# Seven block products for the down-projection of a SwiGLU FFN, and accumulation into DRAM

## The chip, the cores and the metric

One core of a Trainium2 chip runs the kernel. The metric is the device time of one execution in microseconds (us), as the median of several runs. TensorE (PE) multiplies, VectorE (DVE) and ScalarE (ACT) do elementwise work, GpSimd (POOL) and SyncE (SP) mostly issue transfers; 16 DMA engines move the data.

## The reference, cut to what matters

One step of a decoder trunk: a half-step FFN, a mixer of attention and state-space heads, a second half-step FFN and a last norm, over 520 tokens (512 of a prompt, 8 of single-token sequences). Only the two FFNs are touched. All is in float32.

```python
D_MODEL = 1024; D_FF = 2816
def half_ffn(x, norm_g, w_in, w_out):
    h = rmsnorm(x, norm_g)
    gate, up = jnp.split(h @ w_in, 2, axis=-1)
    return x + FFN_RESIDUAL * ((jax.nn.silu(gate) * up) @ w_out)   # FFN_RESIDUAL = 0.5
```

## The kernel before

Activations lie transposed: x is eight tiles of 128 features x 520 tokens, and the 520 tokens are handled as two halves of 260. Each float32 operand of a matmul is cut into a high part (a cast to fp32r on ScalarE) and a low part (a subtraction on VectorE), and a product is three matmuls: high x high, high x low, low x high. `cut` does this for weights, and takes two tiles of the "q" ring; raw weights come by DMA into tiles of the "r" ring.

The hidden width of 2816 is 22 tiles of 128, taken in four parts (`PARTS`): tiles 0 to 5, 6 to 11, 12 to 17, 18 to 21. Within a part the gate and up projections of its tiles come first, then the part's down-projection, which adds 0.5 times its result to x in SBUF (line 468). The first five tiles (`SFROM`) are plain: 96 matmuls each. The others are "pairs": gate and up with two halves of the model width and two token halves are a 2 x 2 block product, done with seven block products in place of eight (`comb_pair`, `comb_last`, 84 matmuls). The seven weight combinations are made from five raw tiles: two of them get their sum by an accumulating DMA from GpSimd's queue (lines 348 and 349), two more by additions on VectorE (lines 381 and 383), and then all seven are cut (lines 354 and 355). The combinations of the activations are made once per FFN by `combos`. The PSUM banks of a pair are called x, y and z; partial sums stay in a bank, are read there by ScalarE or VectorE, and further products are added to them. Product 4 of a pair is issued inside the next pair.

The down-projection (the loop over m in `ffn_comb`) is plain: for each of eight output tiles m, two banks, one for each token half, with (tiles of the part) x 3 matmuls each. Its weights are two raw tiles, 512 and 256 columns wide, for a part of six tiles. The last part of the first FFN takes its weights from the mixer's stream (`w_take`), and the last part of the second FFN is done by `last_out`.

TensorE's instructions run in the order in which the program states them. The other engines' order is worked out by a scheduler when the program is built, with the program's order as priority; on the chip each engine's order is fixed. `stream` lists the weight units with the time each is to cover; `b_more` cuts units until 10 us of work (`AHEAD`) are cut ahead, and `b_split` has raw weights loaded two units ahead. SBUF pools: "pf" (14 q tiles and 12 r tiles), "pg" (12 more q tiles), "p2" (58 general tiles of 528 columns). x is reloaded at the end of part 0, from the input xT in the first FFN and from a DRAM tensor `spill` in the second (the mixer writes its sum there).

## Time and profile before

| | |
|---|---|
| time, median of 3 runs | 1107.76 us (1106.94 to 1111.99) |
| the profiled execution's own time | 1109.26 us |
| its span from first to last instruction | 1107.5 us |
| PE, DVE, ACT, POOL busy in the span | 1073.4, 719.4, 501.4, 264.6 us |
| mean granted TensorE clock | 0.99 of full speed |
| bytes by DMA | 204.30 MB, 184 GB/s in the mean |

The busy time of an engine is the time that at least one of its instructions covers. Instructions can overlap: a matmul's duration runs from its start to its modelled end, and the next one may have started by then. The share of the DMA engines is the mean busy share of 16 engines in a stretch. The first FFN lies at 8 to 376 us, the mixer after it, the second FFN from about 715 us to the end.

### The profile page before, as it was taken

The numbers are of one execution on the slowest core, as the hardware profiler recorded it, in microseconds if no ns is written. First come the engines' busy times: TensorE is split into PE (matmuls) and PEld (weight loads), VectorE is DVE, ScalarE is ACT, GpSimd is POOL, SyncE is SP. The second block draws the span as 40 slices with busy tenths as digits, with TensorE's granted clock in tenths as the row PEclk, the third lists the DMA queues.
The fourth block names the chain that finished last, engine by engine and source line by source line (L and its number), as shares of the span: only waits on it lengthen the run. The fifth ranks groups of instructions, "written<-read, shape, count | busy, mean of one in ns | idle before, by whom it ended". The sixth has DMA issues, their size and how long they took to land.

```text
span 1107.5 us, 23255 instructions
## 1 busy us (share of the span) xinstructions
PE 1073.4 (97%) x9079; PEld 991.7 (90%) x9079; DVE 719.4 (65%) x1499; ACT 501.4 (45%) x1077; POOL 264.6 (24%) x261
## 2 busy tenths in 40 slices
PE   8999999999999999999999998999999999999995
PEld 6999999999999988776756676999999999999995
DVE  6985477467555679363768868449855764685563
ACT  6452355256244422456622555245534543562452
POOL 0001001110105667575343321120020011101013
PEclk9999999999999999999999999999999999999997
DMA  8539358455616788688899735163484584556302
GB/s 272 136 104 255 92 144 222 107 139 170 161 47 205 269 305 298 232 281 305 292 379 406 268 131 197 47 221 99 133 226 104 131 232 98 147 176 150 109 11 78
DMA packets 93917, 204.30 MB, mean 184 GB/s; under 512 B 13384, under 2 KB 21960, under 8 KB 89712
## 3 DMA queue, kind: packets, MB, share of 16 engines
q1 hardware_dynamic: 68736, 124.19, 34.4%
q0 software_dynamic: 22336, 77.08, 24.6%
q10 hardware_dynamic: 2736, 1.56, 0.5%
q8 instruction: 71, 1.16, 0.4%
q14 instruction: 38, 0.31, 0.1%
HBM read 191.78 MB, written 11.01 MB: 183 GB/s over the span
## 4 chain that ended last, share of the span: by engine, by line
PE 86%; DVE 5%; DMA 3%; issue 2%; ACT 2%; POOL 1%; ACTq 0%; DVEq 0%; SPq 0%; POOLq 0%
PE fo L223 7%; PE fo L224 7%; PE fo L222 7%; PE cx L578 6%; PE cx L577 6%; PE cx L576 6%; PE mps L222 4%; PE mps L223 3%; PE mps L224 3%; PE gu L222 3%; PE gu L224 3%; PE gu L223 3%; PE cy L576 3%; PE cy L577 3%; PE cy L578 3%; PE sps L1060 2%
## 5 line engine op out<-in xcount | busy, mean ns | idle before, releaser
L354 ACT CAST qh<-br 128x512 fp32r<-128x512 f32 (+1 forms) x310 | 168.2, 585 | 120.0 <-PE fo L223 57.5
L355 DVE TENSOR_TENSOR ql<-br,qh 128x512 fp32r<-128x512 f32 (+1 forms) x310 | 188.8, 644 | 44.1 <-ACT qh L354 19.3
L223 PE MATMUL fo<-hidl,qh 128*128 128x260 f32 x640 | 181.3, 283 | 0.8 <-DVE hidl L613 0.8
L222 PE MATMUL fo<-hidh,qh 128*128 128x260 f32 x640 | 181.1, 283 | 0.0
L224 PE MATMUL fo<-hidh,ql 128*128 128x260 f32 x640 | 180.8, 283 | 0.0
L578 PE MATMUL cx<-ch,ql 128*128 128x260 f32 x544 | 153.8, 283 | 0.0
L577 PE MATMUL cx<-cl,qh 128*128 128x260 f32 x544 | 153.6, 282 | 0.0
L576 PE MATMUL cx<-ch,qh 128*128 128x260 f32 x544 | 153.5, 282 | 0.0
L223 PEld LDWEIGHTS fo<-hidl,qh 128*128 128x128 f32 x640 | 120.4, 188 | 1.6 <-DVE hidl L613 1.5
L222 PEld LDWEIGHTS fo<-hidh,qh 128*128 128x128 f32 x640 | 120.5, 188 | 0.0
L224 PEld LDWEIGHTS fo<-hidh,ql 128*128 128x128 f32 x640 | 120.5, 188 | 0.0
L222 PE MATMUL mps<-hh,whi 128*128 128x260 f32 x384 | 113.3, 295 | 2.3 <-DVE raw L880 2.3
L348 POOL DMA_DIRECT2D br<-in_wi x34 | 29.7, 874 | 354.7 <-DMA br<-in_wi 204.7
L223 PE MATMUL mps<-hl,whi 128*128 128x260 f32 x384 | 109.7, 286 | 0.6 <-DVE hl L233 0.6
L224 PE MATMUL mps<-hh,wlo 128*128 128x260 f32 x384 | 109.4, 285 | 0.0
L576 PEld LDWEIGHTS cx<-ch,qh 128*128 128x128 f32 x544 | 102.4, 188 | 0.0
L578 PEld LDWEIGHTS cx<-ch,ql 128*128 128x128 f32 x544 | 102.4, 188 | 0.0
L577 PEld LDWEIGHTS cx<-cl,qh 128*128 128x128 f32 x544 | 102.3, 188 | 0.0
L786 POOL DMA_INDIRECT kv<-in_kc,ix x66 | 74.0, 1122 | 59.5 <-PE cy L578 25.7
L222 PEld LDWEIGHTS mps<-hh,whi 128*128 128x128 f32 x384 | 73.3, 191 | 13.5 <-issue 10.4
L577 PE MATMUL cy<-cl,qh 128*128 128x260 f32 x272 | 77.0, 283 | 0.0
L576 PE MATMUL cy<-ch,qh 128*128 128x260 f32 x272 | 76.9, 283 | 0.0
(430 smaller groups left out, 2705.4 us busy)
## 6 DMA issues: line engine op xcount, KB each, us to landing
br<-in_wi SPq DMA_DIRECT2D x206, 256.0 KB, 3.9
br<-in_wi POOLq DMA_DIRECT2D x68, 256.0 KB, 4.7
br<-in_wo SPq DMA_DIRECT2D x56, 256.0 KB, 2.9
wraw<-in_wm SPq DMA_DIRECT2D x24, 512.0 KB, 6.3
br<-in_wo SPq DMA_DIRECT2D x48, 128.0 KB, 2.7
kv<-in_kc SPq DMA_DIRECT2D x22, 256.0 KB, 4.6
spill<-xr SPq DMA_DIRECT2D x16, 260.0 KB, 3.3
xr<-spill SPq DMA_DIRECT2D x16, 260.0 KB, 5.5
```

Of the source, the lines that this page charges most:

```text
L222: mm(out, lhsT=hi[:, ks], rhs=xh[:, cs], start=start, stop=False)
L223: mm(out, lhsT=hi[:, ks], rhs=xl[:, cs], start=False, stop=False)
L224: mm(out, lhsT=lo[:, ks], rhs=xh[:, cs], start=False, stop=stop)
L348: nc.gpsimd.dma_start(s1, u[:, h[1]], accum_op=ALU.add)
L354: self.nc.scalar.copy(hi[:, :n], raw[:, :n])
L355: self.nc.vector.tensor_sub(lo[:, :n], raw[:, :n], hi[:, :n])
L576: mm(out, lhsT=hi[:, ks], rhs=xh, start=start and i == 0, stop=False, skip_group_check=True)
L577: mm(out, lhsT=hi[:, ks], rhs=xl, start=False, stop=False, skip_group_check=True)
L578: mm(out, lhsT=lo[:, ks], rhs=xh, start=False, stop=i == 3, skip_group_check=True)
L786: nc.gpsimd.indirect_dma_start(out=pages[j], out_offset=None, in_=a["kc"], in_offset=bass.IndirectOffsetOnAxis(ap=self.ix[:, 4 * n + j:4 * ...
L1060: nc.tensor.matmul(self.sbank[32 * hp:32 * hp + 32, cs], lhsT=self.qz[:, c0:c0 + 32], rhs=rhs(hp), start=(n % 16 == 0), stop=(n % 16 == 15 ...
```

## The change

The down-projection of the first three parts (`COMB`) is done with seven block products too. Two output tiles m and m + 1, two halves of the part's hidden tiles (three and three) and two token halves are the 2 x 2 blocks. The weights are combined and cut as for the gate/up pairs, 384 columns wide. The hidden tiles are combined in twos by the new `hidden` (the plain first five as well), so that `gate_up2` now returns the uncut product; the rows of `w_ffn_out` are reordered to suit (`hidden_order`). The results no longer go to x in SBUF: they are scaled by 0.5 or -0.5 into tiles of a new pool "px" and added to `spill` in DRAM by accumulating DMAs from GpSimd's queue. In the first FFN xT is copied to `spill` first. x is reloaded from `spill` only in the last part. The down-projection of a part now follows the first gate/up pair of the next part. In the gate/up pairs product 4 of the pair before moves from behind product 6 to behind product 5. The rings shrink: pf 14 to 11 q tiles and 12 to 10 r tiles, pg 12 to 9; px (4) and py (2) are new.

```diff
+COMB = (0, 1, 2)
...
+def hidden_order():
+    o = []
+    for part, (lo, hi) in enumerate(PARTS):
+        o += [j for i in range(2) for j in range(lo + i, hi, 2)] if part in COMB else range(lo, hi)
+    return o
...
+        def down(part):
+            lo, hi = PARTS[part]
+            n = 128 * (hi - lo)
+            w = [wo[m][:, lo * 128:hi * 128] for m in range(8)]
+            if part in COMB:
+                return [("pair", w[m], w[m + 1], n // 2, 1.26 * (hi - lo)) for m in range(0, 8, 2)]
+            return [("dn", w[m], n, 0.72 * (hi - lo)) for m in range(8)]
...
+                if j == lo and part - 1 in COMB:
+                    u += down(part - 1)
...
-        return (self.p0 if first else self.pf).tile([128, 512], F32, name=name, tag="r", bufs=4 if first else 12)
+        return (self.p0 if first else self.pf).tile([128, 512], F32, name=name, tag="r", bufs=4 if first else 10)
...
+                if j == 4:
+                    for _ in range(2):
+                        self.hidden(raw.pop(0), hid)
...
                     if after is not None:
+                        for k in range(8):
+                            nc.sync.dma_start(self.spill[k], self.a["xT"][k])
                         self.setup_cache()
...
+                    if j == lo and todo is not None:
+                        self.down_comb(hx, prev, hid)
+                        hx, todo, prev = [], None, None
...
+                if last:
+                    self.reload(self.spill)
...
+    def down_comb(self, hx, tail, hid):
+        nc = self.nc
+        a, b = slice(0, HF), slice(HF, T)
+        stt = nc.vector.scalar_tensor_tensor
+        for m in range(0, 8, 2):
+            w = self.b_take()
+            x, y, z = (self.bank1(n)[:, :HF] for n in ("dx", "dy", "dz"))
+            x0, x1 = (self.px.tile([128, 528], F32, name=f"xs{m + i}", tag="x") for i in range(2))
+            pu = self.t2("pu")
+            self.product(x, w, 1, True, hx)
+            nc.scalar.copy(z, x)
+            self.product(y, w, 5, True, hx)
+            nc.scalar.activation(pu[:, a], y, AF.Copy, scale=-0.5)
+            if m == 0:
+                self.comb_last(tail, hid)
+            self.product(x, w, 6, False, hx)
+            nc.scalar.activation(pu[:, b], x, AF.Copy, scale=0.5)
+            self.product(z, w, 2, False, hx)
+            nc.scalar.activation(x0[:, a], z, AF.Copy, scale=0.5)
+            self.product(x, w, 7, False, hx)
+            stt(x1[:, b], x, -0.5, pu[:, a], ALU.mult, ALU.add)
+            self.product(y, w, 3, False, hx)
+            stt(x0[:, b], y, 0.5, pu[:, b], ALU.mult, ALU.add)
+            nc.gpsimd.dma_start(self.spill[m], x0[:, :T], accum_op=ALU.add)
+            self.product(x, w, 4, False, hx)
+            nc.scalar.activation(x1[:, a], x, AF.Copy, scale=-0.5)
+            nc.gpsimd.dma_start(self.spill[m + 1], x1[:, :T], accum_op=ALU.add)
+            self.b_more()
...
+    def rings(self):
+        self.enter("pf", 11)
+        self.enter("px", 4)
+        self.enter("pg", 9, "right")
+        self.enter("py", 2, "right")
...
+        if prev is not None:
+            self.comb_last(prev, hid)
+        self.product(z, w, 2, False, self.cx)
+        nc.scalar.activation(c[:, a], z, AF.Silu)
+        self.product(x, w, 6, False, self.cx)
+        nc.scalar.copy(pu[:, b], x)
+        self.product(y, w, 3, False, self.cx)
...
+    def hidden(self, c, hx):
+        nc = self.nc
+        a, b = slice(0, HF), slice(HF, T)
+        if not hx or len(hx[-1]) > 1:
+            hx.append({0: c})
+            return
+        x0, x1 = hx.pop()[0], c
+        p1 = self.t2("p1", F32R)
+        nc.scalar.copy(p1[:, a], x0[:, a])
+        nc.vector.tensor_sub(p1[:, b], x0[:, a], p1[:, a])
+        s, t = self.t2("hs"), self.t2("ht")
+        nc.vector.tensor_sub(s[:, a], x0[:, a], x0[:, b])
+        nc.vector.tensor_sub(s[:, b], x1[:, b], x0[:, b])
+        nc.vector.scalar_tensor_tensor(t[:, a], s[:, b], -1.0, x0[:, a], ALU.mult, ALU.subtract)
+        nc.vector.scalar_tensor_tensor(t[:, b], t[:, a], -1.0, x1[:, a], ALU.mult, ALU.subtract)
+        q = self.two(s, x1, t)
+        cut = lambda i, z: [v[:, z] for v in q[i]]
+        hx.append({1: [p1[:, a], p1[:, b]], 5: cut(0, a), 7: cut(0, b), 2: cut(1, a), 3: cut(1, b), 6: cut(2, a), 4: cut(2, b)})
```

## Rows read from the trace of the kernel before

**Rows 1.** The page's busy times (us, share of the span, instructions), and the granted TensorE clock in 40 slices.

```profile
PE 1073.4 (97%) x9079; PEld 991.7 (90%) x9079; DVE 719.4 (65%) x1499; ACT 501.4 (45%) x1077; POOL 264.6 (24%) x261
...
PEclk9999999999999999999999999999999999999997
```

**Rows 2.** What TensorE waited for, longest first in total: line waited at, releaser, us in total, times, longest.

```profile
PE attps L1035 <- ACT pT L1023: 3.1, 2, 2.4
...
PE fo L223 <- DVE hidl L613: 1.2, 3, 0.5
```

**Rows 3.** Groups of instructions by line: a third of the down-projection's matmuls and its weight loads (busy us, mean ns), and one window of 30 us with counts.

```profile
L222 PE MATMUL fo<-hidh,qh 128*128 128x260 f32 x640 | 181.1, 283 | 0.0
...
L222 PEld LDWEIGHTS fo<-hidh,qh 128*128 128x128 f32 x640 | 120.5, 188 | 0.0
...
300.00:330.00 30.00, 30.00 (x252) 30.00 (x251) 16.79 (x33) 12.02 (x26) 1.73 (x2) 1.00 0.22 54
```

The columns of a window are: its us, busy us and count of PE, PEld, DVE, ACT and POOL, the granted clock, the DMA share and GB/s.

**Rows 4.** TensorE and then ScalarE in order of time inside one gate/up pair: start us, duration us, operation.

```profile
253.48 0.28 PE L578 MATMUL cx<-ch,ql 128*128 128x260 f32 x1
...
255.05 0.37 PE L576 MATMUL cz<-ch,qh 128*128 128x260 f32 x1
255.26 0.28 PE L577 MATMUL cz<-cl,qh 128*128 128x260 f32 x1
...
257.92 0.28 PE L578 MATMUL cx<-ch,ql 128*128 128x260 f32 x1
...
253.57 1.14 ACT L354 CAST qh<-br 128x512 fp32r<-128x512 f32 x2
254.62 0.37 ACT L587 COPY cz<-cx 128x260 f32<-128x260 f32 x1
...
258.24 0.38 ACT L593 COPY pu<-cx 128x260 f32<-128x260 f32 x1 [1.06 <-PE cx L578]
```

**Rows 5.** Groups by line with shapes kept apart, of VectorE and ScalarE (busy us, mean ns), and VectorE in order of time through one gate/up pair.

```profile
L355 DVE TENSOR_TENSOR ql<-br,qh 128x512 fp32r<-128x512 f32 x262 | 171.9, 686 | 39.9 <-ACT qh L354 18.2 <-issue 9.3 <-PE fo L224 6.7
L613 DVE TENSOR_TENSOR hidl<-cg,hidh 128x520 fp32r<-128x520 f32 x34 | 23.8, 699 | 17.1 <-ACT hidh L612 17.0
L355 DVE TENSOR_TENSOR ql<-br,qh 128x256 fp32r<-128x256 f32 x48 | 20.0, 418 | 4.2 <-PE cx L577 2.7 <-ACT qh L354 1.1 <-issue 0.3
...
L354 ACT CAST qh<-br 128x512 fp32r<-128x512 f32 x262 | 153.0, 619 | 96.9 <-PE fo L223 49.1 <-issue 18.8 <-DMA br<-in_wi 16.3
L354 ACT CAST qh<-br 128x256 fp32r<-128x256 f32 x48 | 19.5, 405 | 23.1 <-PE fo L223 8.3 <-DMA br<-in_wi 7.5 <-issue 5.8
...
249.48 0.43 DVE L609 SCALAR_TENSOR_TENSOR cg<-cx,cg 128x260 f32<-128x260 f32 x1 [1.79 <-PE cx L578]
250.60 0.70 DVE L613 TENSOR_TENSOR hidl<-cg,hidh 128x520 fp32r<-128x520 f32 x1 [0.69 <-ACT hidh L612]
...
254.76 3.09 DVE L355 TENSOR_TENSOR ql<-br,qh 128x512 fp32r<-128x512 f32 x5
259.67 0.43 DVE L609 SCALAR_TENSOR_TENSOR cg<-cx,cg 128x260 f32<-128x260 f32 x1 [1.82 <-PE cx L578]
```

**Rows 6.** The start of the first FFN: two windows (columns as in rows 3), and one line of VectorE in order of time, the first sum of tile pair 6.

```profile
30.00:60.00 30.00, 30.00 (x249) 29.91 (x248) 30.00 (x62) 15.71 (x29) 1.95 (x2) 1.00 0.41 110
60.00:90.00 30.00, 30.00 (x252) 30.00 (x252) 23.08 (x48) 15.64 (x35) 0.00 (x0) 1.00 0.56 183
...
97.28 0.69 DVE L381 TENSOR_TENSOR s<-br,br 128x512 f32<-128x512 f32 x1 [6.62 <-DMA br<-in_wi]
```

**Rows 7.** Windows (columns as in rows 3). In the first two only one accumulating transfer of 256 KB ran, in the third three plain ones of 256 KB, in the fourth loads of 256 and 128 KB in turn; the fifth is a long stretch of the first FFN; in the last one many transfers were queued.

```profile
303.00:308.00 5.00, 5.00 (x44) 5.00 (x43) 2.11 (x4) 0.62 (x1) 0.35 (x1) 1.00 0.35 54
315.00:319.00 4.00, 4.00 (x35) 4.00 (x35) 3.54 (x8) 3.50 (x8) 0.00 (x0) 1.00 0.39 68
310.00:315.00 5.00, 5.00 (x44) 5.00 (x43) 1.50 (x3) 2.62 (x7) 0.86 (x1) 1.00 0.49 161
263.00:270.00 7.00, 7.00 (x59) 6.94 (x59) 7.00 (x16) 6.84 (x18) 0.00 (x0) 1.00 0.65 182
120.00:240.00 120.00, 119.51 (x995) 119.27 (x994) 73.58 (x141) 57.28 (x123) 12.97 (x15) 1.00 0.57 147
580.00:606.00 26.00, 24.33 (x207) 16.86 (x209) 22.39 (x52) 7.23 (x20) 7.86 (x8) 1.00 1.02 421
```

**Rows 8.** GpSimd's accumulations (duration ns: least, median, most); DMA issues with the median us from issue to landing; and SP's queue in order of time: two writes to `spill`, and the end of the first FFN's weight loads up to the mixer's first.

```profile
L348 POOL DMA_DIRECT2D br<-in_wi x34: 856/865/1045, 34.7 to 1021.5; - x34
...
br<-in_wi POOLq DMA_DIRECT2D x68, 256.0 KB, 4.7
...
spill<-xr SPq DMA_DIRECT2D x16, 260.0 KB, 3.3
xr<-spill SPq DMA_DIRECT2D x16, 260.0 KB, 5.5
...
309.87 1.28 SPq L347 DMA_DIRECT2D br<-in_wi  x3
337.50 1.29 SPq L165 DMA_DIRECT2D wraw<-in_wo  x3
...
353.71 0.34 SPq L1440 DMA_DIRECT2D spill<-xr  x1
...
356.58 0.33 SPq L1440 DMA_DIRECT2D spill<-xr  x1
```

More of the change, by code (lines that the diff above doesn't have):

```diff
@@ L296, in stream @@
         u = []
-        for lo, hi in PARTS:
+        def down(part):
[5 more added lines that the diff above has]
+            return [("dn", w[m], n, 0.72 * (hi - lo)) for m in range(8)]
+        for part, (lo, hi) in enumerate(PARTS):
             for j in range(lo, hi):
@@ L301, in stream @@
                 else:
-                    u.append(("pair", wi[2 * j], wi[2 * j + 1], 10.1))
-            if s == "1" and hi == PARTS[-1][1]:
-                break
-            u += [("dn", wo[m][:, lo * 128:hi * 128], (hi - lo) * 128, 0.72 * (hi - lo)) for m in range(8)]
+                    u.append(("pair", wi[2 * j], wi[2 * j + 1], 512, 10.1))
+                if j == lo and part - 1 in COMB:
+                    u += down(part - 1)
+            if part not in COMB and not (s == "1" and hi == PARTS[-1][1]):
+                u += down(part)
         self.bu = u
@@ L419, in ffn_comb @@
                         self.leave("p0")
-                        self.enter("pg", 12, "right")
+                        self.enter("pg", 9, "right")
+                        self.enter("py", 2, "right")
                     self.b_more()
@@ L430, in ffn_comb @@
                         r = self.rsq_half2(norm, held)
-                        hid.append(self.gate_up2(*held, r))
+                        raw.append(self.gate_up2(*held, r))
                         held = None
@@ L437, in ffn_comb @@
                 else:
-                    hid.append(self.gate_up2(*pair, r if j < SRAW else None))
+                    raw.append(self.gate_up2(*pair, r if j < SRAW else None))
                 if j == SRAW - 1:
@@ L442, in ffn_comb @@
                     if after is not None:
+                        for k in range(8):
+                            nc.sync.dma_start(self.spill[k], self.a["xT"][k])
                         self.setup_cache()
-            prev = None
+            prev, hx, todo = None, [], None
             for part, (lo, hi) in enumerate(PARTS):
+                last = part == len(PARTS) - 1
+                comb = part in COMB
+                if part:
+                    hid = []
                 for j in range(max(lo, SFROM), hi):
-                    prev = self.comb_pair(j, prev, hid)
-                last = part == len(PARTS) - 1
-                if part == 0:
-                    self.reload(source)
+                    prev = self.comb_pair(j, prev, hx if prev and j == lo else hid, comb)
+                    if part == 0:
+                        for c in raw:
+                            self.hidden(c, hid)
+                    if j == lo and todo is not None:
+                        self.down_comb(hx, prev, hid)
+                        hx, todo, prev = [], None, None
+                if comb:
+                    hx, todo = hid, part
+                    continue
                 tail, prev = prev, None
+                if last:
+                    self.reload(self.spill)
                 if last and after is None:
@@ L486, in to_mixer @@
             self.w_split()
+    def rings(self):
+        self.enter("pf", 11)
+        self.enter("px", 4)
+        self.enter("pg", 9, "right")
+        self.enter("py", 2, "right")
     def enter(self, name, bufs, side="left"):
@@ L548, in combos @@
             c = self.cx[i]
-            c[1] = [t[:, a] for t in self.h[i]]
+            p1 = self.t2("p1", F32R)
+            for z, t in zip((a, b), self.h[i]):
+                nc.scalar.copy(p1[:, z], t[:, a])
+            c[1] = p1[:, a], p1[:, b]
             c[2], c[3] = ([t[:, z] for t in self.h[i + 4]] for z in (a, b))
@@ L567, in combos, with product @@
         halves(self.two(*tt), 6, 4)
-    def product(self, out, w, p, start):
+    def product(self, out, w, p, start, blocks):
         mm = self.nc.tensor.matmul
         hi, lo = w[p]
-        for i in range(4):
-            xh, xl = self.cx[i][p]
+        last = len(blocks) - 1
+        for i, block in enumerate(blocks):
+            xh, xl = block[p]
             ks = slice(128 * i, 128 * i + 128)
@@ L577, in product, with comb_pair @@
             mm(out, lhsT=hi[:, ks], rhs=xl, start=False, stop=False, skip_group_check=True)
-            mm(out, lhsT=lo[:, ks], rhs=xh, start=False, stop=i == 3, skip_group_check=True)
-    def comb_pair(self, j, prev, hid):
+            mm(out, lhsT=lo[:, ks], rhs=xh, start=False, stop=i == last, skip_group_check=True)
+    def comb_pair(self, j, prev, hid, comb):
         nc = self.nc
@@ L1533, in run @@
             self.spill = self.pd.tile([8, 128, T], F32, name="spill")
-            self.enter("pf", 14)
-            self.enter("pg", 12, "right")
+            self.rings()
             self.w_start()
@@ L1595, in run @@
             self.leave("pw")
-            self.enter("pf", 14)
+            self.enter("pf", 11)
+            self.enter("px", 4)
             self.b_limit = len(self.bu)
```

86 lines of the change are left out of this document (40 added, 46 removed).

## The prediction, made before the result was known

> **What bounds the kernel now.** I read the busy shares first, then what TensorE waited for, then how closely its matmuls follow each other, and last the engines and DMA that feed it. TensorE is busy for 97% of the span at full clock, VectorE for 65%, ScalarE for 45% [rows 1]. TensorE's waits are a few microseconds in all, and the only one at a down-projection is 1.2 us in three pieces [rows 2]. So in both FFNs TensorE sets the time, and a matmul less is time won as long as its inputs keep up. What one is worth has to be read with care: a matmul of 260 columns lasts 283 ns, but 252 of them start in 30 us, one each 0.12 us [rows 3]. They overlap, so the price is 0.12 us.
>
> The Trainium skill says that summed matmul time is a poor measure because matmuls are pipelined, and that summed weight-load time is a good one (Perfetto Trace Analysis, section Identifying the Most-Contended Engine). The trace agrees with the first half; by the second the removed matmuls would be worth 216 x 0.188 = 40.6 us, but the loads overlap too (252 loads of 188 ns would need 47 us of those 30), so the sum below doesn't use it.
>
> **The change: matmuls removed.** Down-projection of one part before: 8 tiles m x 2 token halves x 6 hidden tiles x 3 = 288. After: 4 pairs of m x 7 products x 3 blocks x 3 = 252. 36 less, in three parts of two FFNs: 216 x 0.12 = 25.9 us, all on TensorE's path. A pair of output tiles then takes 63 x 0.12 = 7.6 us in place of 8.6.
>
> **Hand-offs in PSUM.** The plain form evacuates two banks that nothing needs again soon. A new pair uses three banks over and over: product 6 may not enter bank x before the copy of x to z is done, product 7 not before pu is read from x, product 4 not before x1 is read from x. Each time one product of 9 matmuls, 1.08 us, lies between. The nearest rows are those of the gate/up pairs, with 12 matmuls (1.44 us) between: bank x is complete at 253.76, ScalarE is in two casts and starts the copy only at 254.62 (0.86 us late), and the first matmul into z is held by 0.09 us (0.21 to the next start, not 0.12); where ScalarE is idle it starts 0.04 us after the last matmul (257.92 + 0.28 to 258.24) [rows 4]. With 0.36 us less cover, the same lateness would cost 0.09 + 0.36 = 0.45 us, and a prompt start nothing. There are 24 x 3 = 72 such places: 0 to 32 us. I take 5, near the prompt end, since lateness up to 0.41 us is covered and a cast of 384 columns that is already running leaves at most 0.51 us to wait, on average half. The gate/up order also changes: comb_last now stands between product 5 and product 2, which wins up to 34 x 0.09 = 3 us at z, and one product instead of two covers product 7's wait; ScalarE starts that copy at once in the row, so nothing is lost. I take 1 us won.
>
> **VectorE and ScalarE.** A cut of 512 columns is 0.69 us on VectorE and 0.62 on ScalarE, of 256 columns 0.42 and 0.41; so 384 columns cost about 0.55 and 0.51 [rows 5]. A new weight pair has 7 cuts and two adds, and two evacuations on VectorE: 7 x 0.55 + 2 x 0.55 + 2 x 0.43 = 5.8 us; on ScalarE, with copies of 0.37 [rows 4], 7 x 0.51 + 5 x 0.37 = 5.4; both below 7.6. For the hidden tiles, each two of them now need five VectorE steps of 260 columns and three of 520, 5 x 0.43 + 3 x 0.70 = 4.3 us, against 2 x 0.70 before. By pitch (five cuts in a row take 3.09 us, so successive ones start some 0.08 us sooner than the duration says) that is about 1.2 us more for each gate/up pair; VectorE stood idle for 1.8 + 0.7 = 2.5 us of each 10.2 us pair [rows 5]. About 1.3 us stay, so VectorE rises to some 87% there and the q ring, cut from 26 to 20 tiles (14 per unit), still lets cuts run most of a unit ahead. No steady loss; if the cover goes, each microsecond over costs 30 pairs x 1 us.
>
> **The start of each FFN.** VectorE is full there (30.00 of 30 us) and then 23 of 30 [rows 6]. Tile pair 6 is now multiplied right after pair 5, at about 81 us instead of after eight down tiles, while in the trace its sums wait for data until 97.28 [rows 6]. Its loads move ahead of the down weights, into a stretch where DMA has room, and its 5.6 us of VectorE work take the place of down cuts done there now. 0 to 2 us for each FFN; I take 1 in all.
>
> **DMA.** An accumulating transfer of 256 KB alone takes 0.35 x 5 = 1.75 and 0.39 x 4 = 1.56 us of all 16 engines, three plain ones 0.49 x 5 = 2.45, so 1.65 and 0.82 us each [rows 7]. Alternating 256 and 128 KB loads take 4.55 us for 1.27 MB, 1.4 us per 384 KB; 192 KB then costs about 0.7. A gate/up pair costs 5 x 0.82 + 2 x 1.65 = 7.4 us of DMA. Check on before: a part is 6 x 7.4 + 8 x 1.4 = 55.6 us of DMA in 6 x 10.2 + 8 x 4.3 = 95.6 us, 0.58; the windows say 0.57 [rows 7]. A new weight pair costs 5 x 0.7 + 2 x 1.3 = 6.1, and its two accumulations into x in DRAM, for which the trace has no row, at least 2 x 0.82 (plain) and I take 2 x 1.65 (the accumulation into SBUF also reads a sum and writes it); twice that is the other bound. So 9.4 us (7.7 to 12.7) for 7.6 us of TensorE: DMA falls behind inside a down stretch. Over a part it is 6 x 7.4 + 4 x 9.4 = 82 us in 6 x 10.1 + 4 x 7.6 = 91, 0.90. In the 30 us of a stretch the loads that must arrive (half of pair 2, pair 3, the next gate/up pair and half of another, 20 us) and seven accumulations (11.6 us) make 32 us; the raw ring of 10 tiles, two units, gives some 4 us of lead. I take 0.5 us lost per stretch, 3 us in all; 0 if all is covered.
>
> **Queues.** GpSimd issues the accumulations at 0.87 us each, four per new pair, 3.5 of 7.6 us [rows 8]. Weight accumulations stand behind output accumulations there; an output one waits for evacuations and lands some 4.7 us after issue, the four x buffers of two pairs give 15 us. Output accumulations to one m are a part apart; those to different m needn't wait for each other: writes to the same DRAM tensor start 2.87 us apart though one lands in 3.3 [rows 8]. Eight copies of xT to DRAM on SP's queue (FFN1) fall where DMA share is 0.41. The reload of x moves to the end: eight transfers of 0.82 us, first landing 5.5 us after issue, on an SP queue that is empty from 311 to 337 us [rows 8]; 0 to 6 us, I take 0.
>
> **Sum.** -25.9 + 5 - 1 + 1 + 3 = -17.9 us. The profiled execution is 1109.26 us (span 1107.5), 1.5 above the median of 1107.76; 1109.3 - 17.9 = 1091.4, so 1090 us as a median.
>
> **Rivals.** (1) The hand-offs are late as at 253.76 in nearly all places: 72 x 0.45 = 32 us at most, 26 us at 0.36; the gain is gone, about 1108 us. For it: one such place is in the rows, and the casts stand ahead in ScalarE's order. Against: casts are shorter and half the evacuations in the rows start at once. (2) DMA becomes the bound in the down stretches: 9.4 us or, at the dearer accumulation, 12.7 per pair instead of 7.6, over 24 pairs 43 to 122 us lost, 6 x 4 us of it covered: 1090 - 3 + 19 to 98, 1106 to 1185; taking 10.7 (accumulation at 2.3 us), 24 x 3.1 - 24 = 50 lost, 1137 us. It turns the gain into a loss from 25.9 / 24 = 1.1 us lost per pair. For it: the share stands at 1.02 over 26 us where many transfers are queued and doesn't go beyond [rows 7], and accumulations move half as fast as loads. Against: the part as a whole asks for only 0.90. (3) The output accumulations are made to wait for each other's landing: 2 x 4.7 + 2 x 0.87 = 11.1 us per pair in GpSimd's queue, 24 x 3.5 = 84 us lost, 1174; [rows 8] speak against it.
>
> The Trainium skill has a rule that speaks for rival 2: DMAs from all queues run on the same 16 engines and interleave, so GpSimd's queue gives no bandwidth of its own (DMA: Bandwidth & Descriptors, section Issuing engines are not separate DMA queues). The trace agrees, with the share that stops near 1.0 in [rows 7] whichever queues are busy.
>
> **How the numbers follow.** My forecast, 1082 to 1101 us: 0.66. Rival 1, within half a percent: 0.15. Rival 2: 0.13, of which 0.01 still faster and 0.02 within. Rival 3: 0.03. Other losses over 0.5%: 0.03. About 0.5% is what a measurement here can tell from no change: faster is below 1102, slower above 1113. Faster 0.67, same 0.17, slower 0.16. The range reaches from 1081 (every cost at its low end: 1108 - 26 - 3 would be 1079, which takes all of them at once) to 1120, into rival 2; about 0.05 is left out below and 0.12 above.
>
> **What the profile after would show.** 216 fewer matmuls, down pairs 7.6 us apart; first matmuls of products 6, 7 and 4 without long pauses (rival 1: 0.3 us and more before them, behind casts on ScalarE); DMA share about 0.9 over parts 2 and 3, with TensorE unbroken (rival 2: share 1.0 in down stretches, VectorE's sums or ScalarE's casts waiting for loads, TensorE behind them); GpSimd not waiting from one output accumulation to the next (rival 3). The prediction is wrong if TensorE has more than 20 us of new pauses, or if pitch 0.12 us doesn't hold for products of 9.

## The result and the profile after

The changed kernel takes 1118.44 us (median of 5 runs, 1113.40 to 1119.80) against 1107.76 us: ratio 1.0085, 95% interval 1.0063 to 1.0107. It is slower by 0.85%, where 1.6% faster was forecast. A second measurement of it gave 1119.11 us (ratio 1.0096, 1.0081 to 1.0111). The profiled execution took 1118.44 us, its span is 1116.7 us against 1107.5.

The busy times of the page, to be held against [rows 1]: the 216 matmuls are gone, VectorE and ScalarE have more to do, and none is near its full span except TensorE.

```profile
PE 1060.8 (95%) x8863; PEld 971.9 (87%) x8863; DVE 807.5 (72%) x1679; ACT 597.2 (53%) x1321; POOL 348.5 (31%) x357
```

What TensorE waited for (line, releaser, us in total, times, longest; a releaser is the instruction or transfer that ended the wait). In [rows 2] the down-projection had 1.2 us in three pieces. Now its wait is the largest of all, and it is for one instruction: the evacuation of line 533, which must read bank x before product 4 may be added there.

```profile
PE dx L647 <- DVE xs L533: 20.0, 11, 5.0
PE stp L1345 <- DVE xdd L1342: 3.5, 2, 1.9
```

**Where the time went.** I cut the trace at the first matmul of each stretch and call "lost" what a stretch takes beyond its count of matmuls x 0.1197 us (an unbroken gate/up stretch of the second FFN has 492 in 58.88 us). From first to last matmul the two FFNs together took 739.6 us before and 745.2 after, the mixer between them 358.1 and 362.5; the rest is 0.8 us less. The first FFN takes 9.9 us longer than before, the second 4.3 us less. 25.9 us of matmuls went away, the six down stretches lose 30.7 us where the old ones lost 1.9, and the rest of the FFNs loses 2.7 more (1.4 of it at the first output tile of the first FFN's last part). In the down stretches the pause before product 4 makes up 22.7 us, nearly all of it in the third and fourth pair of each four. The first matmuls of products 6, 2 and 7 start 1.3 us late in all. The second matmuls of products 6, 7 and 4 start 0.06 to 0.11 us late in 60 of 72 places, 5.5 us in all, and at the full granted clock but for one, as here at a product 7 (start, duration; 0.19 us from the first to the second, then 0.12):

```profile
96.24 0.36 PE L647 MATMUL dx<-ch,qh 128*128 128x260 f32 x1
96.43 0.28 PE L648 MATMUL dx<-cl,qh 128*128 128x260 f32 x1
96.55 0.28 PE L649 MATMUL dx<-ch,ql 128*128 128x260 f32 x1
```

So the hand-offs of the banks (waits until another engine has read what further matmuls are to be added to) cost 6.8 us, and 5 to 7 us in most of the other kernels below, whatever their rings and transfers. Most of the remaining 1.2 us (0.9) are slower matmuls behind a pause, as in these rows (start, duration, idle before):

```profile
324.08 0.56 PE L647 MATMUL dx<-ch,qh 128*128 128x260 f32 x1 [5.03 <-DVE xs L533]
324.43 0.42 PE L648 MATMUL dx<-cl,qh 128*128 128x260 f32 x1
324.65 0.42 PE L649 MATMUL dx<-ch,ql 128*128 128x260 f32 x1
...
327.47 0.34 PE L647 MATMUL cx<-p,qh 128*128 128x260 f32 x1
327.64 0.28 PE L648 MATMUL cx<-p,qh 128*128 128x260 f32 x1
```

After 5.03 us of idleness matmuls start 0.22 us apart, not 0.12, up to 327.47. The granted clock is 0.50 from 324.20 to 327.40, the lower of the two clock levels (1.2 of 2.4 GHz), and it adds some 1.6 us behind this pause (15 matmuls in 3.39 us), part of them after the end of the stretch.

**Why line 533 is late.** VectorE around that pause (start, duration, idle before). It evacuates bank x at 323.61, 0.42 us long. But in its fixed order cuts and sums for the next gate/up pair stand ahead, and these wait for data, or for casts that wait for data.

```profile
307.65 0.69 DVE L402 TENSOR_TENSOR s<-br,br 128x512 f32<-128x512 f32 x1 [2.44 <-DMA br<-in_wi]
...
316.40 0.69 DVE L402 TENSOR_TENSOR s<-br,br 128x512 f32<-128x512 f32 x1 [1.73 <-DMA br<-in_wi]
...
322.39 1.29 DVE L375 TENSOR_TENSOR ql<-br,qh 128x512 fp32r<-128x512 f32 x2 [3.37 <-ACT qh L374]
323.61 0.42 DVE L533 SCALAR_TENSOR_TENSOR xs<-dx,pu 128x260 f32<-128x260 f32 x1
```

One step back ScalarE's cast waits for a raw tile, and GpSimd's accumulation, which is to follow a plain load, waits for that load:

```profile
321.75 1.14 ACT L374 CAST qh<-br 128x512 fp32r<-128x512 f32 x2 [4.63 <-DMA br<-in_wi]
```

```profile
308.84 0.87 POOL L368 DMA_DIRECT2D br<-in_wi  x1 [0.63 <-DVE ql L375]
317.08 0.88 POOL L369 DMA_DIRECT2D br<-in_wi  x1 [7.37 <-DMA br<-in_wi]
317.62 1.23 POOL L536 DMA_DIRECT2D spill<-xs  x1
```

The windows of that stretch and of another (us, busy us and count of PE, PEld, DVE, ACT and POOL, clock, DMA share, GB/s), against [rows 7]:

```profile
284.00:290.00 6.00, 6.00 (x53) 6.00 (x52) 5.52 (x13) 3.46 (x10) 0.86 (x1) 1.00 0.48 139
290.00:296.00 6.00, 6.00 (x49) 5.65 (x48) 4.47 (x10) 3.36 (x9) 1.68 (x2) 1.00 0.76 163
296.00:302.00 6.00, 6.00 (x50) 5.81 (x49) 4.40 (x9) 3.87 (x10) 2.64 (x4) 1.00 1.01 207
302.00:308.00 6.00, 6.00 (x51) 5.98 (x50) 2.51 (x6) 4.40 (x12) 2.51 (x4) 1.00 1.09 304
...
314.00:320.00 6.00, 5.06 (x40) 4.59 (x38) 3.26 (x5) 2.85 (x7) 2.67 (x3) 1.00 0.81 246
320.00:326.00 6.00, 1.92 (x9) 1.92 (x10) 2.57 (x5) 1.14 (x2) 2.00 (x3) 0.85 1.09 180
...
840.00:870.00 30.00, 27.90 (x226) 27.39 (x226) 20.72 (x39) 18.31 (x41) 11.43 (x13) 1.00 1.08 258
```

The down stretch begins at 285.42. DMA is half idle around that time (share 0.48), is full from 296 us on but for one window of 0.81, and TensorE stops when the stretch is nearly over. (A share above 1 means that packet times on an engine overlap.) SP's queue (start, length, count) begins to load for the next gate/up pairs only at 294.33 and takes 29 us over 15 loads. From 285 to 326 us it waited longest for VectorE's cuts, which free the raw tiles (releaser, us in total, times, longest):

```profile
285.59 8.09 SPq L367 DMA_DIRECT2D br<-in_wo  x7
294.33 29.11 SPq L367 DMA_DIRECT2D br<-in_wi  x15
...
SPq L367 <- DVE ql L375: 29.7, 13, 6.8
```

So far this is read from one trace. My theory is that weights come late because the transfers of a down stretch start late and are then more than the DMA engines move in time. The runs take its two halves apart. The expectations call the first half C (loads start too late for want of free raw tiles) and the second A (too much DMA work, the output accumulations above all); B is the rival that the place of the output accumulations in GpSimd's fixed order does the harm.

### The profile page after: what moved, and what is told of

Read it like the earlier page. It is cut to its first block, busy times and chain, and to the rows that moved or that the text cites. A ratio compares the mean times of both kernels' runs of the same rounds, so it can differ in the third digit from the quotient of the medians.

```text
span 1116.7 us, 23740 instructions
## 1 busy us (share of the span) xinstructions
PE 1060.8 (95%) x8863; PEld 971.9 (87%) x8863; DVE 807.5 (72%) x1679; ACT 597.2 (53%) x1321; POOL 348.5 (31%) x357
## 3 DMA queue, kind: packets, MB, share of 16 engines
q0 software_dynamic: 36160, 99.31, 37.2%
## 5 line engine op out<-in xcount | busy, mean ns | idle before, releaser
L647 PE MATMUL cx<-ch,qh 128*128 128x260 f32 x408 | 115.6, 283 | 1.7 <-ACT pu L666 1.7
L648 PE MATMUL cx<-cl,qh 128*128 128x260 f32 x408 | 115.1, 282 | 0.0
L649 PE MATMUL cx<-ch,ql 128*128 128x260 f32 x408 | 115.1, 282 | 0.0
L375 DVE TENSOR_TENSOR ql<-s,qh 128x512 fp32r<-128x512 f32 (+1 forms) x116 | 72.1, 631 | 22.0 <-ACT qh L374 7.7
L647 PE MATMUL dx<-ch,qh 128*128 128x260 f32 x216 | 66.8, 309 | 20.1 <-DVE xs L533 20.0
L374 ACT CAST qh<-s 128x512 fp32r<-128x512 f32 (+1 forms) x116 | 66.7, 575 | 29.4 <-PE cx L649 10.7
L647 PEld LDWEIGHTS cx<-ch,qh 128*128 128x128 f32 x408 | 76.7, 188 | 2.2 <-ACT pu L666 2.1
L649 PE MATMUL cy<-ch,ql 128*128 128x260 f32 x272 | 76.8, 283 | 0.0
L233 PEld LDWEIGHTS mps<-hl,whi 128*128 128x128 f32 x384 | 74.6, 194 | 1.2 <-DVE hl L243 1.1
L234 PEld LDWEIGHTS mps<-hh,wlo 128*128 128x128 f32 x384 | 74.5, 194 | 0.5 <-DVE wlo L202 0.5
```

Of the source, the lines that this page charges most:

```text
L233: mm(out, lhsT=hi[:, ks], rhs=xl[:, cs], start=False, stop=False)
L234: mm(out, lhsT=lo[:, ks], rhs=xh[:, cs], start=False, stop=stop)
L374: self.nc.scalar.copy(hi[:, :n], raw[:, :n])
L375: self.nc.vector.tensor_sub(lo[:, :n], raw[:, :n], hi[:, :n])
L647: mm(out, lhsT=hi[:, ks], rhs=xh, start=start and i == 0, stop=False, skip_group_check=True)
L648: mm(out, lhsT=hi[:, ks], rhs=xl, start=False, stop=False, skip_group_check=True)
```

## The experiments

"Lost" is that of the six down stretches in us, "wait" TensorE's for line 533 (a few lines lower in the spread kernels), "FFNs" and "mixer" as above; the last four come from one execution each, which can lie up to 6 us from the median. The ratio is to the kernel before, beside which each was timed.

| kernel | median us | ratio, 95% interval | FFNs | mixer | lost | wait |
|---|---|---|---|---|---|---|
| before | 1107.76 | | 739.6 | 358.1 | (1.9) | |
| changed | 1118.44 | 1.0085 (1.0063 to 1.0107) | 745.2 | 362.5 | 30.7 | 20.0 |
| e19_after_again (the same) | 1119.11 | 1.0096 (1.0081 to 1.0111) | 751.3 | 359.3 | 35.0 | 21.0 |
| e1_no_out | 1098.06 | 0.9907 (0.9871 to 0.9942) | 730.2 | 359.6 | 15.3 | 5.7 |
| e7_plain_out | 1108.43 | 0.9998 (0.9982 to 1.0013) | 739.7 | 362.2 | 23.6 | 12.4 |
| e14_ring9 | 1130.78 | 1.0207 (1.0177 to 1.0236) | 764.5 | 355.9 | 45.7 | 26.4 |
| e2_ring (11) | 1104.09 | 0.9968 (0.9945 to 0.9991) | 735.3 | 354.9 | 21.9 | 11.2 |
| e11_ring13 | 1106.95 | 0.9990 (0.9974 to 1.0006) | 733.3 | 362.2 | 13.3 | 4.0 |
| e12_ring15 | 1108.40 | 0.9994 (0.9971 to 1.0017) | 728.4 | 372.9 | 10.3 | 2.0 |
| e18_px3_r12 | 1112.42 | 1.0030 (1.0006 to 1.0055) | 749.0 | 359.0 | 29.6 | 17.7 |
| e15_spread | 1104.27 | 0.9967 (0.9940 to 0.9995) | 737.6 | 357.0 | 24.7 | 11.4 |
| e16_spread_r11 | 1093.06 | 0.9862 (0.9807 to 0.9917) | 726.7 | 355.5 | 12.8 | 2.7 |
| e17_spread3_r11 | 1094.35 | 0.9878 (0.9837 to 0.9919) | 728.4 | 355.2 | 10.5 | 0.8 |

The others: e3_dve_sums 1129.26 (1.0218), e5_act_evac 1124.69 (1.0167), e9_pool_sums 1106.61 (0.9990), e13_pool_ring13 1150.07 (1.0379); and of the kernel before, e4_rings_before 1108.64 (1.0008), e10_pool_before 1111.45 (1.0043).

The same program differs from one execution to the next: the two profiles of the changed kernel are 3.1 us apart in the mixer, 6.1 in the FFNs and 4.3 in "lost" (3.6 of these 4.3 are matmuls at the lower clock). So differences of that size in one row are not read as effects. The mixer's length goes largely with TensorE's granted clock: it is at the lower level for 3.4 us of the mixer in e2 (354.9 us), for 6.8 in the kernel before (358.1), 13.7 in the changed one (362.5) and 27.3 in e12 (372.9). Why it falls more often in some executions is not shown.

### What the output accumulations cost

e1 leaves the 48 accumulations into x out, so that the result lacks parts 1 to 3 of both FFNs; e7 turns them into plain writes, so that the sum is not formed.

```diff
# e1: lines 536 and 539 become pass; e7:
-            nc.gpsimd.dma_start(self.spill[m], x0[:, :T], accum_op=ALU.add)
+            nc.gpsimd.dma_start(self.spill[m], x0[:, :T])
```

> The changed kernel without its 48 accumulating transfers into x in DRAM (the sums are formed and dropped, so the FFNs' first three parts are missing from the output). Theory A: the pauses before product 4 (20.0 us of waits for VectorE's evacuation of bank x) come from VectorE's fixed order, in which the first sum of the next gate/up pair's weights stands ahead of that evacuation and waits for a weight transfer that is late because the output accumulations fill the 16 DMA engines. Then the wait falls from 20 to under 6 us, the DMA share of the down stretches from 1.04 to 1.08 to under 0.85, and the time to 1093 to 1102 us. Theory B: the weights are late because the rings of raw and cut tiles shrank. Then the wait stays at 15 us or more and the time at 1112 to 1119 us.

> The output accumulations become plain writes to the same place (so spill keeps only the last part written; the FFNs' results are then not the full sum). Same instructions in the same places of GpSimd's queue, but half the DMA work (about 0.8 in place of 1.7 us per transfer). Theory A (DMA work): about half of what leaving them out gave back, 1105 to 1111 us, TensorE's wait for line 533 at 8 to 14 us. Rival B (their places in GpSimd's fixed order delay the weight accumulations behind them, whatever they move): 1115 to 1119 us, wait near 20.

GpSimd's queue in the DMA part of the page (packets, MB, share of 16 engines), of the changed kernel, e1 and e7:

```profile
q0 software_dynamic: 36160, 99.31, 37.2%
```

```profile
q0 software_dynamic: 29248, 86.52, 30.9%
```

```profile
q0 software_dynamic: 33088, 99.31, 33.3%
```

37.2% of 1116.7 us less 30.9% of 1098.4 is 76 us, 1.58 us for each of 48 accumulations; 33.3% of 1112.4 less the same is 31 us, 0.65 for a plain write. (The loads on the other queue took 11 us more in e1; with them the accumulation comes to 1.35.) Without the accumulations TensorE runs almost unbroken through the window that begins as far behind the start of its stretch as the one at 840 us above, with DMA at 0.89 (e1; same columns as above), a little more than the 0.85 of the expectation:

```profile
829.30:859.30 30.00, 29.93 (x245) 29.58 (x245) 22.55 (x42) 19.71 (x43) 6.35 (x8) 1.00 0.89 227
```

With less than half the DMA work for the outputs, in the same places of GpSimd's queue, e7 gets back 10.0 of the 20.4 us that e1 gave back, as theory A expected, and not the nothing of B. So the work counts, and the place in the queue alone is out; that the place has a part in the rest is not excluded.

### Is it one badly placed evacuation, or the smaller rings?

e5 moves line 533's reading of bank x to ScalarE; e4 gives the kernel before the smaller rings of the changed one (11 and 9 q tiles, 10 raw tiles).

```diff
# e5
-            stt(x1[:, b], x, -0.5, pu[:, a], ALU.mult, ALU.add)
+            nc.scalar.activation(x1[:, b], x, AF.Copy, scale=-0.5)
+            nc.vector.tensor_add(x1[:, b], x1[:, b], pu[:, a])
```

> The changed kernel with the evacuation of bank x before product 4 moved from VectorE to ScalarE (a scaled copy; VectorE adds pu afterwards in SBUF, where no bank waits for it). DMA work is unchanged. Theory A: TensorE no longer stands behind VectorE's queue; waits at product 4 fall from 20 to under 6 us, the DMA share in down stretches stays at 1.0, and the time is 1097 to 1106 us. If ScalarE's queue is held in the same way, by its casts of late sums, half of the waits come back under ScalarE's name and the time is 1107 to 1112. Theory C: DMA is the bound outright, TensorE would wait for the weights themselves; the time stays at 1113 to 1119 us.

> The kernel before with the smaller rings of the changed one (pf 11 and pg 9 cut tiles, 10 raw tiles), nothing else. Theory A: within 3 us of 1107.8, TensorE as busy as before in both FFNs. Theory B: the rings cost by themselves, 1113 us or more.

e5 came out slower, which I had not expected. The down stretches lose only 12.8 us, but the pauses turn up in the next gate/up pairs, where no evacuation was touched:

```profile
PE cx L647 <- DVE pu L671: 13.1, 5, 4.7
PE dx L647 <- ACT xs L533: 5.9, 2, 5.7
```

So the data are late; which instruction TensorE is seen to wait for is only a matter of what stands behind them on VectorE or ScalarE. e4 shows that the rings alone cost the old kernel nothing that can be measured (0.08%, interval -0.07 to 0.22).

### Less DMA for the weight sums

e3 makes the two sums of a down pair on VectorE from raw tiles; e9 makes them for all pairs on GpSimd; e10 does e9's edit in the kernel before; e13 is e9 with 13 raw and 56 general tiles and another order of loads.

```diff
# e9, e10
-        for d, src in ((g0, g[:, h[0]]), (s1, u[:, h[0]]), (g1, g[:, h[1]]), (s3, u[:, h[0]]), (u1, u[:, h[1]])):
+        for d, src in ((u1, u[:, h[1]]), (s3, u[:, h[0]]), (g0, g[:, h[0]]), (g1, g[:, h[1]])):
             nc.sync.dma_start(d, src)
-        nc.gpsimd.dma_start(s1, u[:, h[1]], accum_op=ALU.add)
-        nc.gpsimd.dma_start(s3, g[:, h[0]], accum_op=ALU.add)
+        nc.gpsimd.tensor_add(s1, s3, u1)
+        nc.gpsimd.tensor_add(s3, s3, g0)
```

> The changed kernel with the two sums of each down weight pair formed by VectorE from the raw tiles (two additions of 384 columns more for each pair) and not by accumulating DMA; one plain load and two accumulations fewer for each of 24 pairs, about 3.3 of 9.4 us of DMA. Theory A: the share in down stretches falls to 0.75 to 0.9, waits at product 4 to under 8 us, the time to 1095 to 1104 us. Theory C as well, with no waits for VectorE left. Theory B: no change, 1112 to 1119 us. If VectorE's two more additions count, the waits stay though the DMA share falls.

> The changed kernel, but the two weight sums that were accumulating transfers are additions on GpSimd from raw tiles (1.29 us for 512 columns, from its additions elsewhere in the trace), so a weight pair needs four plain loads and no accumulation: by the rows 3.3 in place of 7.4 us of DMA for a gate/up pair, some 2.8 in place of 6.1 for a down pair. The ring of raw tiles stays at ten, five for each pair. Theory A: the pauses of the down stretches go, 1090 to 1098 us. Rival C (late start of loads because of the ring): the pauses stay above half, 1105 to 1115. A further case, D: GpSimd's additions slow VectorE (one row of VectorE's 512-column cut above 0.75 us in place of 0.69) and so the whole: above 1118.

> The kernel before with the same two sums on GpSimd. There the loads are no bound by theory A: 1105 to 1109 us. Were it faster by more than 5 us, the sums' transfers would have cost the old kernel too and the gain of e9_pool_sums would not be the change's own loss given back.

> Weight sums by additions on GpSimd as in e9_pool_sums, with the tile that is cut first loaded first, and 13 raw tiles with 56 general ones. In e9_pool_sums the pauses at product 4 fell from 22.7 to 3.6 us, but 7 us came up at the start of the FFNs and 5 us at product 7 behind casts on ScalarE. If these too were raw tiles that came late: 1092 to 1098 us. If GpSimd's additions (1.3 us each, behind output accumulations that wait for evacuations in its fixed order) are what is late: 1100 to 1107.

e3 missed: less DMA, and slower. The wait for line 533 rises to 25.6 us, as in the last case of its expectation, but the cuts and sums around its pauses wait for data as before. In the stretch that begins at 289.52 us there, DMA is mostly idle at first (same columns):

```profile
290.00:296.00 6.00, 5.80 (x49) 5.59 (x48) 5.71 (x13) 4.55 (x12) 0.00 (x0) 1.00 0.44 132
296.00:302.00 6.00, 5.93 (x49) 5.71 (x48) 5.35 (x12) 2.75 (x7) 1.75 (x2) 1.00 0.32 68
```

A reason may be that its sums hold the raw tiles longer; no run shows that apart. It is the first sign that the sum of the transfers does not decide alone. e9 gave back 12 us and halved what is lost (15.9 us), though the same edit made the kernel before slower (e10, 0.43%; its 1111.45 us lie above the 1105 to 1109 expected), but it did not reach its 1090 to 1098. VectorE's cuts of raw tiles became slower, as the first half of case D had it; the time above 1118 us did not come:

```profile
L375 DVE TENSOR_TENSOR ql<-br,qh 128x512 fp32r<-128x512 f32 x214 | 172.7, 827 | 18.6 <-ACT qh L374 8.8 <-PE cy L648 3.0 <-PE cx L648 1.7
```

against 688 ns in the changed kernel. In order of time, GpSimd and then VectorE in e9:

```profile
952.25 1.29 POOL L368 TENSOR_TENSOR br<-br,br 128x512 f32<-128x512 f32 x1 [3.59 <-DVE ql L375]
953.61 1.62 POOL L369 TENSOR_TENSOR br<-br,br 128x512 f32<-128x512 f32 x1
```

```profile
951.47 0.69 DVE L375 TENSOR_TENSOR ql<-br,qh 128x512 fp32r<-128x512 f32 x1 [0.64 <-ACT qh L374]
952.08 0.42 DVE L668 TENSOR_TENSOR cg<-cy,pu 128x260 f32<-128x260 f32 x1
952.63 1.46 DVE L375 TENSOR_TENSOR ql<-br,qh 128x512 fp32r<-128x512 f32 x1
954.01 0.42 DVE L671 TENSOR_TENSOR pu<-cx,pu 128x260 f32<-128x260 f32 x1
954.53 1.00 DVE L672 SCALAR_TENSOR_TENSOR cg<-pu,cg 128x260 f32<-128x260 f32 x1
```

While GpSimd adds, a cut takes 1.46 us, not 0.69, and line 672 takes 1.00, while line 671, of the same size but with one input in PSUM, keeps its 0.42. Over all 34 pairs line 672 rises from a median of 427 ns in the changed kernel to 996 in e9, line 671 goes from 420 to 417. The Trainium skill says that VectorE and GpSimd share a pair of SBUF ports as an exclusive lock, which a VectorE operation with two SBUF inputs needs against a GpSimd operation that reads SBUF (SBUF — State Buffer, section SBUF: two separate sides); the trace agrees, with line 672 slowed and line 671 not. e13 missed by over 40 us: its cuts of sums rose to 1.0 us in the mean, and TensorE's wait for line 533 came back (22.7 us). Why its order is so much worse than e9's I have not settled.

### When the loads can start

One line: the count of raw tiles. 13 and 15 take two and four of the 58 general tiles for it.

```diff
-        return (...).tile([128, 512], F32, name=name, tag="r", bufs=4 if first else 10)
+        return (...).tile([128, 512], F32, name=name, tag="r", bufs=4 if first else 11)    # 9, 13, 15
```

> Nine raw tiles, one fewer than in the changed kernel. Theory C: the other direction of e2_ring, 1125 to 1140 us, and TensorE's wait for line 533 above 28 us. If 11 tiles helped only by another order of VectorE's instructions and not by their lead: 1112 to 1122.

> The changed kernel with 11 raw tiles in place of 10. Theory A (the 16 DMA engines have too much to move in and around a down stretch, the output accumulations included): the work is the same, 1115 to 1119 us. Rival C (the raw loads start too late, because a tile must first come free; DMA stands idle before and is full after): one tile more starts a load about a cut earlier, 1109 to 1114 us, and the 20.0 us that TensorE waits for the evacuations of line 533 fall below 15.

> The changed kernel with 13 raw tiles in place of 10, at the price of two of the 58 general tiles. One tile more gave 14 us (1104.09). Theory C (raw loads start too late, because a tile of the ring must come free first): three tiles more give back most of what TensorE still waits for line 533 (11.2 us with 11 tiles), 1093 to 1099 us, wait under 5 us. Theory A alone (the DMA engines have more to move than a down stretch has time for): the lead gets longer, but the transfers still take 9.4 us for each 7.6 us pair, so some pauses stay: 1099 to 1104, wait 5 to 11. If two general tiles fewer stall the combinations of the hidden tiles: above 1104.

> 15 raw tiles (three whole pairs), 54 general tiles. Theory C: as with 13 or up to 3 us better, 1091 to 1098. Theory A: 1097 to 1103. If the general tiles become the bound: slower than with 13, waits of VectorE or ScalarE for matmuls that still read the old combinations.

The loss goes 45.7, 30.7, 21.9, 13.3, 10.3 us for 9, 10, 11, 13 and 15 tiles, with the same transfers; some 6 us of each are the hand-offs. The loads are earlier indeed: the last load for the first down pair of a stretch is issued 19.1 us before the pair's first matmul with 10 tiles, 28.4 with 13, 32.3 with 15 (means of six). What TensorE waits for line 533, with 9, 11 and 13:

```profile
PE dx L647 <- DVE xs L533: 26.4, 11, 5.1
```

```profile
PE dx L647 <- DVE xs L533: 11.2, 7, 2.9
```

```profile
PE dx L647 <- DVE xs L533: 4.0, 2, 3.8
```

The waits are those of theory C, but for 9 tiles, where I had put over 28 us; the 14 us that the 11th tile gave are more than it had expected, and 7.6 us of the difference between the two profiles lie in the mixer. How full DMA is does not tell the kernels apart: with 15 tiles the share in a stretch rises as with 10, to 1.09, and TensorE runs through (same columns):

```profile
932.00:962.00 30.00, 30.00 (x249) 29.74 (x248) 22.48 (x41) 19.76 (x44) 11.47 (x13) 1.00 1.09 278
```

The times of 13 and 15 lie above both theories. With 13 that is the range of the third case, that fewer general tiles cost something, but its FFNs are no longer than with 11 tiles; its mixer is 7.3 us longer. With 15 the time differs from that with 13 by less than the intervals, so its third case is not shown. With 15 the FFNs are 16.8 us shorter than in the changed kernel, but the mixer is 10.4 us longer: its wait on line 1342 is 8.6 us against 3.5, and its matmuls run at the lower clock for 27.3 us against 13.7. That the four general tiles that it lost are the cause I have not shown. e18 tries 12 raw tiles and keeps the general ones:

> 12 raw tiles, paid for by one of the four tiles that hold results on their way to DRAM, all 58 general tiles kept; order as in the changed kernel. If the general tiles are what 13 and 15 raw tiles lost again: 1096 to 1102 us. If three result tiles are too few (an accumulation lands 7 us after its issue): above 1104, evacuations waiting for accumulations to land.

Its second case came: three result tiles are too few, and VectorE now waits for one to be written out:

```profile
L533 DVE SCALAR_TENSOR_TENSOR xs<-dx,pu 128x260 f32<-128x260 f32 x24 | 10.2, 427 | 20.8 <-DMA spill<-xs 18.6 <-PE dy L648 2.0
```

In the changed kernel these transfers take a median of 7.0 us from issue to landing (row of the DMA issues):

```profile
spill<-xs POOLq DMA_DIRECT2D x48, 260.0 KB, 7.0
```

### Apart from each other

e15 keeps all rings and all transfers, but puts two down pairs behind each of the next part's first two gate/up pairs; e16 adds the 11th raw tile; e17 has groups of one, one and two. The combinations of the hidden tiles of these gate/up pairs wait until the down pairs are done.

```diff
-                if j == lo and part - 1 in COMB:
-                    u += down(part - 1)
+                if j - lo < 2 and part - 1 in COMB:
+                    u += down(part - 1)[2 * (j - lo):2 * (j - lo) + 2]
...
-                    if j == lo and todo is not None:
-                        self.down_comb(hx, prev, hid)
-                        hx, todo, prev = [], None, None
+                    if todo is not None:
+                        self.hold = [] if j == lo else self.hold
+                        self.down_comb(hx, prev, hid, 4 * (j - lo), 4 * (j - lo) + 4)
+                        prev = None
+                        if j - lo == 1:
+                            hx, todo, hold, self.hold = [], None, self.hold, None
+                            for c in hold:
+                                self.comb_done(c, comb, hid)
```

> The changed kernel with its rings (10 raw tiles), but the four down pairs of a part follow the first two gate/up pairs of the next part, two after each, and the hidden tiles of these two are combined after the last of them. By the rows a down pair asks for 9.4 us of DMA in 7.6 us and a gate/up pair for 7.4 in 10.1: four in a row are 7.2 us behind, two are 3.6 and win back 2.7 before the next two. Burst theory: about half of the 30.6 us that the down stretches lose comes back, 1100 to 1107 us. Steady lack (the same transfers, the same ring): 1115 to 1121. A third case: the combinations of four half-tiles of hidden at once (some 9 us of VectorE) come late for the next products: above 1121.

> The same with 11 raw tiles. Burst theory: the two remedies add up in part, 1092 to 1099 us, less than 10 us lost in the down stretches. Steady lack: as e2_ring, 1102 to 1106.

> Down pairs in groups of one, one and two behind the first three gate/up pairs, 11 raw tiles. Burst theory: as e16 or up to 4 us better, 1089 to 1098 us. If keeping the old combinations of hidden tiles for one more gate/up pair takes too many general tiles: slower than e16, waits in front of matmuls for the hidden tiles' combinations.

All three times lie within what the burst theory gave, but e16 loses 12.8 us where under 10 was expected; 6.7 of them are the hand-offs. By itself e15 does not show it, though: its loss fell by a fifth and not by half (30.7 to 24.7 us; 5.5 of its 14 us stand in the mixer). With 11 tiles the same edit shows clearly: e2 and e16 are 9.1 us apart in the loss and 8.6 in the FFNs. In e16 a window of one stretch, and the fullest 30 us of the second FFN:

```profile
925.00:955.00 30.00, 29.31 (x241) 28.85 (x240) 24.01 (x45) 20.21 (x43) 8.81 (x10) 1.00 0.99 237
...
840.00:870.00 30.00, 30.00 (x248) 29.66 (x248) 25.36 (x48) 20.25 (x43) 8.24 (x10) 1.00 1.04 246
```

The share is 0.99 and 1.04 where it was 1.08, and TensorE runs almost without a break. e16 is faster than both kernels: 1093.06 us, 1.4% (0.8 to 1.9%) below the kernel before. The Trainium skill says that where a kernel has regimes with different busiest engines, interleaving them may help (Perfetto Trace Analysis, section Optimization Strategy); this pair of runs agrees, with the 11 us from e2 to e16.

> The changed kernel as it is, to have a second profile of it. If the 4.4 us in the mixer belong to the change: the mixer takes 362 to 363 us again and the median is 1117 to 1120. If the mixer changes from one execution to the next, as the times of each kernel spread over 6 to 12 us: another length, 355 to 361 us, while the down stretches lose 30.6 us again, to within 1 us.

The down stretches lost 35.0 us, so they do not repeat to within 1 us, against what I had expected; the mixer took 359.3. So the mixer's 4.4 us are not a fixed part of the change.

## Why the prediction was wrong

**The step that failed** is the last of the DMA part: that a raw ring of two units "gives some 4 us of lead", so that late data cost "0.5 us lost per stretch, 3 us in all". The pauses before product 4 and the lower clock behind them cost 23.6 us, 3.9 per stretch. The price beneath it was about right: 1.65 us was taken for an output accumulation, 1.58 measured (1.35 by the other count). The demand was of the right size too: the shares of 0.93 in the 40.8 us of the stretch at 285 and of 0.99 in the 35.3 us of that at 824 make 38 and 35 us of all engines, where 32 was worked out for 30 us. What failed is the lead. The ring did not let the loads run far enough ahead: in the stretch at 285 us SP's queue waited 29.7 us for VectorE's cuts to free raw tiles, and the DMA share was 0.69 and 0.78 in its first two windows of 6 us. It is the same there with 15 tiles (0.69 and 0.89), yet that kernel loses a third of what this one does: the share does not show how far ahead of its use a load is issued, and the runs with 9 to 15 tiles show that this counts.

**Rival 2 came true**, near the low end of its price: 19 to 98 us were given for it, 23.6 found, 1.0 us for each of 24 pairs. That is just below the 1.1 at which it was said to turn the gain into a loss by itself; the hand-offs and the 2.7 us in the rest of the FFNs do the remainder. It was given 0.13, because a part as a whole asks for 0.90. A mean over 90 us says nothing of a burst of 30 us if the ring between holds only two units. Its other sign, a share that "doesn't go beyond" 1.02, was read too strictly: it reaches 1.09 in the changed kernel.

**The other terms.** Matmuls: 216 x 0.12 = 25.9 us, and pitch 0.12 holds for products of 9 (e16, 248 in 30.00 us). Hand-offs: 5 us taken, 4.8 found at products 6, 2 and 7 (1.3 at their first matmuls, 3.5 at the second ones of 6 and 7), and 2.0 more at the second matmul of product 4. Rival 1 is out: it had 26 to 32 us in 72 places, and it is the long pauses before product 4, which go with DMA work and raw tiles, that make the loss. Rival 3 is out: in the changed kernel two output accumulations start 0.54 us apart in GpSimd's queue, and before the second of a pair (line 539) the queue waited 0.8 us in the sum of all 24 cases, and not for a transfer. Start of the FFNs and gate/up order: 0 taken together, 1.1 lost (plain tiles lose 1.1 less, pairs 2.2 more). The expected view, a share of about 0.9 with TensorE unbroken, is nearer to e16 (0.88 from 803 to 989 us) than to the change.

**Open.** The first FFN's down stretches lose twice what the second's do (20.3 and 10.4 us), though their down pairs are the same; that is what turns the gain of the second FFN into a loss of the whole, and I have not found why. How much of the loss is DMA work and how much the wait for free tiles can't be divided, because either remedy alone works: without the accumulations 15.3 us are left at 10 tiles, with them 13.3 at 13 tiles, of which some 6 each are hand-offs.

## What to carry to other kernels

Set the transfers of a stretch against its own time and ask when the first of them can start: a ring holds only so many loads ahead of their use, and a full DMA stops TensorE or not according to that lead (1.08 with pauses at 10 tiles, 1.09 without at 15). When a step gets faster and more costly in transfers at once, don't put its pieces in a row; between slower work their transfers can use what that work leaves over (e16). And where several engines run in a fixed order, the instruction that TensorE waits for is often the last of a chain: moving it (e5) moved the pause and did not remove its cause.

## What the runs showed of the hardware that I had not expected

- An accumulating transfer of 260 KB from SBUF into DRAM takes 1.58 us of all 16 DMA engines (1.35 if the other queue's change is counted), a plain one 0.65. In the changed kernel it lands 7.0 us (median) after its issue; with three result tiles in place of four VectorE waited 18.6 us for such landings.
- Additions on GpSimd (1.29 us alone, 2.01 in the mean at line 368 in e9) and VectorE's operations on two SBUF tiles slow each other: 688 to 827 ns in the mean for the 512-column cuts of raw tiles, 1.46 us for one that fell beside an addition, 427 to 996 ns (medians) for line 672; line 671, with an input in PSUM, keeps its 0.42 us.
- A pause of 5 us in TensorE was followed by matmuls 0.22 us apart for 3.4 us, at a granted clock of 0.50.
- Products 6, 7 and 4 go on in bank x after another engine has read it; their second matmul starts 0.06 to 0.11 us late in 60 of 72 places, 5.5 us in six stretches.
